# Walking the moving weights of a matmul from the last column to the first in a 256-token decoder trunk

## The chip, the cores and the metric

The kernel runs on one core of one Trainium2 chip. The metric is the device time of one execution in microseconds (us); the median of three runs stands for a kernel. Where single instructions are looked at, times are in nanoseconds (ns). Engines are named as the profile names them: PE is TensorE (matrix multiply), PEld is its weight load, DVE is VectorE, ACT is ScalarE, SP is SyncE, whose queue issues most of the transfers.

## The reference

A decoder trunk of two layers on 256 tokens of width 2048, all in float32. Layer 0 mixes tokens by trailing-window pooling, layer 1 by causal attention over the tokens (with 256 tokens there is one block, so it is plain causal attention). Both have a second branch, a 4-head attention into 256 memory tokens.

```python
for i in range(DEPTH):                                   # 2 layers
    if i == N_A_LAYERS:                                  # before layer 1
        k_blocks, v_blocks, k_mean = moba_shared_kv(h, w_kv_shared)
    u = h @ w_in[i]
    branch_in, gate_b, mem_q, gate_m = jnp.split(u, split_at, axis=-1)
    if i < N_A_LAYERS:
        branch = multiscale_pool(branch_in, pool_w[i], pool_scale[i])
    else:
        branch = moba_attention(branch_in, k_blocks, v_blocks, k_mean)
    mem_o = memory_attention(mem_q, mem, w_mem_kv[i])
    mixed = jnp.concatenate([branch * silu(gate_b), mem_o * silu(gate_m)], axis=-1)
    y = mixed @ w_out[i]
    h = layer_norm(DEEPNORM_ALPHA * h + y, ln_g[i], ln_b[i])
```

## The kernel before

Every float32 factor is split into a high part in the matmul's reduced float32 type and a rest (`split`, lines 70 to 73: ACT writes the high part, DVE the rest). A product is then three matmuls: high by high, high by rest, rest by high. All of them go through the helper `mm` (line 67), so all stand under L68 in the profile and are told apart by their tiles. In a matmul on PE one operand is loaded into the array first (stationary, 128 columns, an LDWEIGHTS of its own on PEld that runs while the matmul before it runs), the other is streamed through it column by column (moving, up to 512 columns), and as many columns of output go to a bank of PSUM.

The weights come from memory in blocks of 128 x 1024 (512 KB), the `items`. `run` (line 131) walks the list of items: it loads an item four ahead, splits it three ahead, and calls its `consume`, which records the matmuls. The order in which the items stand is written out by hand; PE gets one item's matmuls after the other.

There are two kinds of projection:

- `proj_t` (line 168): the weights are stationary (128 columns of `wh` or `wl`), the activations `xT` or `memT` move. Each pair is a matmul of 512 columns (high and rest of the activations side by side) and one of 256. Keys, queries, gates and pool inputs are made this way: 2688 matmuls, `acc<-xm,wh` and `acc<-xm,wl` in the profile.
- `proj_n` (line 194): 128 columns of the activations are stationary, the weights move, 512 columns at a time. Each item gives 12 matmuls (two halves of the tokens, two blocks of the inner dimension, three products). Memory values (`mem_v`), the values of layer 1 (`w_sv`) and the output projections (`w_out`) are made this way.

The last 512 columns of the last output projection are kept in SBUF and multiplied at the end by `last` (line 732), in one pass of 512 columns for the first half of the tokens, and in two of 256 for the second.

Where the operands lie: `xT` and `memT` are parts of one tile `xm`, both shifted by `SHIFT` = 40 columns (160 bytes) against its start. The weights' tiles `wh`, `wl`, the mixed activations `zT`, and the kept columns `kept` (also in `xm`, but from its start) are not shifted. `w_sv` is split into the place of `memT` (`in_mem`, line 651), and so is shifted like `xT`.

By stage, the matmuls with moving weights are:

- `mem_v`, both layers: 192 of 512 columns, stationary `memT` (shifted), moving `wh`, `wl` (not shifted); tiles `xm` with `wh` or `wl`, into `pt`, `o` and `acc`.
- `w_sv`: 288 of 512 columns, stationary `xT` and moving values both in `xm`, both shifted; `acc<-xm`.
- `w_out` of layer 0 (384) and of layer 1 (288), 512 columns, stationary `zT`, moving `wh`, `wl`, neither shifted; `acc<-wh,zT` and `acc<-wl,zT`.
- `last`: 48 of 512 columns and 96 of 256, stationary `zT`, moving `kept`, neither shifted; `acc<-xm,zT`.

Of the kernel before, what the change touches and what calls it, by code (L numbers as in the profile page):

```python
# [20 lines left out]
KT = D // P  # L21
# [25 lines left out]
def trunk(ctx: ExitStack, tc: tile.TileContext, a: dict, out: bass.AP):  # L47
# [11 lines left out]
    kept = [xm[:, i * KX:(i + 1) * KX].rearrange("p (k n) -> p k n", k=KT) for i in range(2)]  # L59
# [7 lines left out]
    def mm(o, l, r, start, stop):  # L67
        nc.tensor.matmul(o, l, r, start=start, stop=stop)  # L68
# [17 lines left out]
    def item(src, cols, consume=None, dst=None):  # L86
        items.append(dict(src=src, cols=cols, consume=consume, dst=dst, cuts=(0, cols)))
# [106 lines left out]
    def proj_n(sta, wblk, done, korder=range(8), banks=("acc", "acc"), place=None):  # L194

        acc = []
        korder = list(korder)

        def consume(j, kb):
            def go(wh, wl):  # L200
                if j == 0:
                    acc.extend(ps.tile([P, 512], F32, name=b, bufs=4 if b == "acc" else 1) for b in banks)
                h = wh.rearrange("p (k n) -> p k n", n=512)
                l = wl.rearrange("p (k n) -> p k n", n=512)
                for t in range(2):
                    for kk in range(2):
                        k = 2 * kb + kk
                        xh = sta[:, k, t * P:(t + 1) * P]
                        xl = sta[:, k, T + t * P:T + (t + 1) * P]
                        first, last = j == 0 and kk == 0, j == 7 and kk == 1  # L210
                        mm(acc[t], xh, h[:, kk], first, False)
                        mm(acc[t], xh, l[:, kk], False, False)
                        mm(acc[t], xl, h[:, kk], False, last)
                    if j == 7:
                        done(t, acc[t])
            return go
        for j, kb in enumerate(korder):
            item(wblk[kb], BLK, consume(j, kb), dst=place and ("keep", *place(j)))
# [34 lines left out]
    def heads_tile(name):  # L253
        return sb.tile([P, 4, 2 * T], F32R, name=name)
# [202 lines left out]
    def fresh(key, make):  # L457

        tiles = []

        def g():
            if not tiles:
                tiles.append(make())
                st[key] = tiles[0]
            return tiles[0]
        return g
# [189 lines left out]
    for grp in range(3):  # L656
        k = fresh("k", lambda: heads_tile("kk"))
# [74 lines left out]
    def last(t, c0, c1):  # L732
        o = ps.tile([P, 512], F32, name="acc", bufs=4)[:, :c1 - c0]
        for k in range(KT):
            zh = zT[:, k, t * P:(t + 1) * P]
            zl = zT[:, k, T + t * P:T + (t + 1) * P]
            mm(o, zh, kept[0][:, k, c0:c1], k == 0, False)
            mm(o, zh, kept[1][:, k, c0:c1], False, False)
            mm(o, zl, kept[0][:, k, c0:c1], False, k == KT - 1)
        return o  # L740

    def add(t, c0, c1, o):
# [21 lines left out]
    def store(t, c0, c1):  # L764
        nc.sync.dma_start(out[t * P:(t + 1) * P, c0:c1], res[:, t, c0:c1])

    o = last(0, 0, 512)
    nc.vector.bn_aggr(m0, stats[:, 1, :3].rearrange("p a b -> p (a b)"))
    for n in (1, 2):
        times_g(n)  # L770
    add(0, 0, 512, o)
    norm_stats(0, 4)
    o = last(1, 0, 256)
    finish(0, 0, 1)
    add(1, 0, 256, o)
    finish(0, 2, 3)
    o = last(1, 256, 512)
# [85 lines left out]
```

## Time and profile before

| | us |
|---|---|
| three runs | 822.35, 823.62, 823.64 |
| median | 823.62 |
| profiled execution | 823.66 |
| its span, first to last instruction | 821.9 |
| PE busy | 812.0 |
| PEld busy | 702.3 |
| DVE busy | 558.5 |
| ACT busy | 396.0 |

A row of the chain of waits has start, duration, engine, tile, line and a count of instructions merged into it. A row of a timeline has start, duration, engine, line, operation, output and inputs, shape and count. The length of one matmul in a row (389 ns for 512 columns) is from its start to the end of its modelled drain; matmuls overlap, so the time that one takes of PE is the distance from one start to the next, called pitch here. It is had from a merged row by dividing its length by its count. A row by windows has for each stretch its length, then for each engine the busy time with the number of instructions that touch it, then the granted TensorE clock (1.00 is full speed), the DMA share and the rate in GB/s.

### The profile page before, as it was taken

To read this page: it belongs to the slowest core of one execution; us is meant where nothing else is said; L and a number is where in the kernel's file an instruction comes from. 1 tells how busy PE (TensorE), PEld (TensorE's weight loads), DVE (VectorE), ACT (ScalarE), POOL (GpSimd) and SP (SyncE) were. 2 spreads that over 40 slices of the span, in tenths; PEclk is the share of its full clock that TensorE was granted. 3 is DMA by queue.
4 is the path that set the end of the run, shared out by engine and by line. 5 is a ranking of instruction groups with operands and counts; after the bars stand their busy time and mean duration, and the time that the engine had idled before them with its cause. 6 is when DMAs were issued, how large, how long until landed. Compare 5 with 4: busy or idle time off the path is not lost.

```text
span 821.9 us, 11533 instructions
## 1 busy us (share of the span) xinstructions
PE 812.0 (99%) x4444; PEld 702.3 (85%) x4444; DVE 558.5 (68%) x794; ACT 396.0 (48%) x578; POOL 0.2 (0%) x4
## 2 busy tenths in 40 slices
PE   9999999999999999999999999999999999999996
PEld 6888898898888888888898888888888888888885
DVE  5686668657957555697667667566765667658746
ACT  6564545545545434445465445454554445545520
POOL 0000000000000000000000000000000000000000
PEclk9999999999999999999999999999999999999998
DMA  8866555557558666676654554656555555637842
GB/s 324 302 232 205 168 165 180 180 163 227 180 176 292 207 201 192 199 237 197 201 157 152 189 170 157 206 158 198 179 166 168 182 188 167 209 127 232 278 130 103
DMA packets 47164, 159.15 MB, mean 194 GB/s; under 512 B 5375, under 2 KB 7167, under 8 KB 46847
## 3 DMA queue, kind: packets, MB, share of 16 engines
q1 hardware_dynamic: 45792, 155.21, 58.0%
q10 hardware_dynamic: 1316, 3.19, 1.0%
q8 instruction: 35, 0.57, 0.3%
q14 instruction: 21, 0.17, 0.1%
HBM read 156.28 MB, written 2.10 MB: 193 GB/s over the span
## 4 chain that ended last, share of the span: by engine, by line
PE 98%; DVE 1%; DMA 0%; ACT 0%; issue 0%; DVEq 0%; SPq 0%
PE acc L68 89%; PE o L68 4%; PE s L68 2%; PE pt L68 2%; PE pt L363 0%; DMA raw<-in_w_mk 0%; PE pt L313 0%; DVE res L806 0%; PE pt L638 0%; PE o L638 0%; DVE res L787 0%; DVE stats L745 0%; DVE res L744 0%; ACT wh L72 0%; DVEq L859 0%
## 5 line engine op out<-in xcount | busy, mean ns | idle before, releaser
L68 PE MATMUL acc<-xm,wh 128*128 128x512 f32 x1344 | 468.7, 395 | 0.5 <-ACT wh L72 0.5
L73 DVE TENSOR_TENSOR wl<-raw,wh 128x1024 fp32r<-128x1024 f32 (+2 forms) x250 | 295.0, 1186 | 150.0 <-ACT wh L72 149.1
L68 PE MATMUL acc<-xm,wl 128*128 128x256 f32 x1344 | 363.3, 280 | 0.0
L72 ACT ACTIVATE wh<-raw 128x1024 fp32r<-128x1024 f32 (+2 forms) x250 | 255.3, 1028 | 187.3 <-PE acc L68 133.3
L68 PEld LDWEIGHTS acc<-xm,wh 128*128 128x128 f32 x1344 | 248.3, 189 | 49.8 <-ACT wh L72 1.5
L68 PEld LDWEIGHTS acc<-xm,wl 128*128 128x128 f32 x1344 | 253.6, 189 | 7.4 <-DVE wl L73 0.4
L68 PE MATMUL acc<-wh,zT 128*128 128x512 f32 x448 | 140.0, 390 | 0.0
L68 PEld LDWEIGHTS acc<-wh,zT 128*128 128x128 f32 x448 | 84.1, 188 | 17.3
L68 PE MATMUL acc<-wl,zT 128*128 128x512 f32 x224 | 87.2, 389 | 0.0
L68 PE MATMUL acc<-xm 128*128 128x512 f32 x288 | 65.8, 389 | 0.0
L68 PEld LDWEIGHTS acc<-xm 128*128 128x128 f32 x288 | 54.1, 188 | 11.2
L73 DVE TENSOR_TENSOR xm<-raw,xm 128x1024 fp32r<-128x1024 f32 (+2 forms) x41 | 47.7, 1171 | 20.6 <-ACT xm L72 20.4
L221 ACT ACTIVATE fold<-acc 128x256 f32<-128x256 f32 x72 | 27.7, 385 | 62.3 <-PE acc L68 61.1
L72 ACT ACTIVATE xm<-raw 128x1024 fp32r<-128x1024 f32 (+2 forms) x41 | 41.3, 1014 | 19.6 <-PE acc L68 9.8
L68 PEld LDWEIGHTS acc<-wl,zT 128*128 128x128 f32 x224 | 42.1, 188 | 8.5
L222 DVE TENSOR_TENSOR fold<-acc,fold 128x256 f32<-128x256 f32 x72 | 29.4, 418 | 5.4 <-ACT fold L221 5.4
L72 ACT ACTIVATE zT<-zf 128x256 fp32r<-128x256 f32 x32 | 12.9, 414 | 39.6 <-DVE zf L283 35.3
L68 PE MATMUL acc<-xm,zT 128*128 128x256 f32 (+1 forms) x144 | 22.6, 318 | 0.0
L68 PEld LDWEIGHTS acc<-xm,zT 128*128 128x128 f32 x144 | 20.7, 190 | 1.9
L68 PE MATMUL acc<-wh,xm 128*128 128x512 f32 x64 | 21.6, 403 | 0.0
L72 ACT ACTIVATE ph<-pt 128x384 fp32r<-128x384 f32 (+1 forms) x20 | 10.7, 535 | 22.2 <-PE pt L363 13.5
L73 DVE TENSOR_TENSOR zT<-zf,zT 128x256 fp32r<-128x256 f32 x32 | 12.8, 422 | 9.7 <-ACT zT L72 9.7
(124 smaller groups left out, 503.6 us busy)
## 6 DMA issues: line engine op xcount, KB each, us to landing
raw<-in_w_in SPq DMA_DIRECT2D x128, 512.0 KB, 3.5
raw<-in_w_out SPq DMA_DIRECT2D x64, 512.0 KB, 4.3
raw<-in_w_sk SPq DMA_DIRECT2D x24, 512.0 KB, 4.5
raw<-in_w_sv SPq DMA_DIRECT2D x24, 512.0 KB, 3.3
raw<-in_w_mv SPq DMA_DIRECT2D x14, 512.0 KB, 5.6
raw<-in_w_mk SPq DMA_DIRECT2D x12, 512.0 KB, 3.3
raw<-in_xT SPq DMA_DIRECT2D x4, 512.0 KB, 4.8
res<-in_x ACTq DMA_DIRECT2D x2, 1024.0 KB, 5.4
```

The lines of the kernel that those rows point to most:

```text
L68: nc.tensor.matmul(o, l, r, start=start, stop=stop)
L72: nc.scalar.activation(hi, src, AF.Copy)
L73: nc.vector.tensor_sub(lo, src, f(hi))
L221: nc.scalar.activation(dst, acc[:, T:], AF.Copy)
L222: nc.vector.tensor_add(dst, acc[:, :T], dst)
```

## The change

In `proj_n` and in `last` the moving operand and the output are given with their columns in reverse: the matmul reads the weights from the last column to the first and writes its output from the last column to the first. Each output column is still the product of the same weight column, and lands at the same address. The stationary operand, the count and the order of the instructions, their waits, and `proj_t` are as before; on every engine the same instructions stand in the same order.

```diff
@@ proj_n, consume
-                        mm(acc[t], xh, h[:, kk], first, False)
-                        mm(acc[t], xh, l[:, kk], False, False)
-                        mm(acc[t], xl, h[:, kk], False, last)
+                        o = acc[t][:, ::-1]
+                        mm(o, xh, h[:, kk, ::-1], first, False)
+                        mm(o, xh, l[:, kk, ::-1], False, False)
+                        mm(o, xl, h[:, kk, ::-1], False, last)
@@ last
-            mm(o, zh, kept[0][:, k, c0:c1], k == 0, False)
-            mm(o, zh, kept[1][:, k, c0:c1], False, False)
-            mm(o, zl, kept[0][:, k, c0:c1], False, k == KT - 1)
+            h, l = (w[:, k, c0:c1][:, ::-1] for w in kept)
+            mm(o[:, ::-1], zh, h, k == 0, False)
+            mm(o[:, ::-1], zh, l, False, False)
+            mm(o[:, ::-1], zl, h, False, k == KT - 1)
```

## Rows read from the trace of the kernel before

**Rows 1.** The page: busy time and share of the span, and the chain by engine.

```profile
PE 812.0 (99%) x4444; PEld 702.3 (85%) x4444; DVE 558.5 (68%) x794; ACT 396.0 (48%) x578; POOL 0.2 (0%) x4
...
PE 98%; DVE 1%; DMA 0%; ACT 0%; issue 0%; DVEq 0%; SPq 0%
```

**Rows 2.** Who waited for whom, PE: waited for, us in total, times, longest.

```profile
PE pt L794 <- DVE cc L791: 2.8, 1, 2.8
PE pt L68 <- DVE zT L126: 1.2, 1, 1.2
PE acc L68 <- ACT wh L72: 0.5, 1, 0.5
PE acc L68 <- ACT cct L796: 0.4, 1, 0.4
```

**Rows 3.** Chain of waits in order of time: output projection of layer 1 and last columns.

```profile
735.09 76.88 PE acc L68 x384
```

**Rows 4.** Busy time by windows, PE alone, inside the 256-column matmuls of `last`.

```profile
802.00:811.00 9.00, 9.00 (x77) 1.00 0.25 93
```

**Rows 5.** Chain of waits: values of layer 1, behind two pieces of `proj_t`.

```profile
505.40 27.35 PE acc L68 x128
...
600.77 27.35 PE acc L68 x128
```

**Rows 6.** Chain of waits: `mem_v` of layer 1, two items and one.

```profile
364.72 5.60 PE acc L68 x24
...
370.76 2.80 PE acc L68 x12
```

**Rows 7.** Chain of waits: `proj_t`, one item and four.

```profile
498.12 2.78 PE acc L68 x16
...
677.40 11.12 PE acc L68 x64
```

**Rows 8.** Timeline of PE, first matmuls of `proj_t` and where their pace changes.

```profile
6.16 0.63 PE L68 MATMUL acc<-xm,wh 128*128 128x512 f32 x1
6.58 0.41 PE L68 MATMUL acc<-xm,wl 128*128 128x256 f32 x1
6.80 0.63 PE L68 MATMUL acc<-xm,wh 128*128 128x512 f32 x1
...
8.72 0.63 PE L68 MATMUL acc<-xm,wh 128*128 128x512 f32 x1
...
10.25 0.28 PE L68 MATMUL acc<-xm,wl 128*128 128x256 f32 x1
10.37 0.39 PE L68 MATMUL acc<-xm,wh 128*128 128x512 f32 x1
```

**Rows 9.** Groups of matmuls with moving weights, shapes apart: busy us, mean ns.

```profile
L68 PE MATMUL acc<-wh,zT 128*128 128x512 f32 x448 | 140.0, 390 | 0.0
L68 PE MATMUL acc<-wl,zT 128*128 128x512 f32 x224 | 87.2, 389 | 0.0
L68 PE MATMUL acc<-xm 128*128 128x512 f32 x288 | 65.8, 389 | 0.0
...
L68 PE MATMUL acc<-xm,zT 128*128 128x256 f32 x96 | 11.7, 283 | 0.0
...
L68 PE MATMUL acc<-xm,zT 128*128 128x512 f32 x48 | 11.0, 389 | 0.0
```

**Rows 10.** Busy time by windows, all engines (PE, PEld, DVE, ACT, POOL): output projection of layer 1.

```profile
735.00:800.00 65.00, 65.00 (x288) 53.83 (x288) 45.28 (x54) 30.30 (x32) 0.00 (x0) 1.00 0.63 210
```

**Rows 11.** Who waited longest between 735 and 800 us.

```profile
ACT wh L72 <- DMA raw<-in_w_out: 12.8, 12, 2.9
```

**Rows 12.** Busy time by windows, PE alone: the highest transfer rate of those read.

```profile
10.00:12.00 2.00, 2.00 (x13) 1.00 1.00 405
```

**Rows 13.** Chain of waits from the last matmul of `last` to the last instruction.

```profile
811.99 0.43 DVE res L744
...
817.94 0.39 DVE res L806
```

## The prediction

> **What bounds the kernel now.** I read the page first: PE is busy for 812.0 us of a span of 821.9, and the chain that ended last is 98% PE [rows 1]. Then the waits: PE waits four times in the whole span, 4.9 us in sum, at its very start and in the tail [rows 2]. So nothing feeds PE too slowly; the time is the sum of the pitches of 4444 matmuls, plus the tail behind the last of them, some 10 us with little PE work in it [rows 13]. The profiled execution took 823.66 us, 1.8 more than its span and 0.04 more than the median of the runs, so a saving in the span is one in the median.
>
> The question is then what sets a pitch. Full speed is 2.4 GHz, a column in 0.417 ns: 512 columns are 213.3 ns and 256 are 106.7. What the rows give:
>
> - 256 columns in the last columns: 77 matmuls touch a stretch of 9.00 us, and each lasts 283 ns, so the pitch is (9.00 + 0.283) / 77 = 120.6 ns; I use 120 [rows 4, 9]. That is 13.3 over the columns.
> - 512 columns in the output projection and the last columns: the row of 384 matmuls holds 288 of 512 columns and these 96; (76.88 - 96 x 0.120) / 288 = 226.9 ns, 13.6 over the columns [rows 3].
> - Values: the row of 128 holds 32 of `proj_t` at 2.78 us for 16, and 96 of the values: (27.35 - 5.56) / 96 = 227.0 ns, 13.7 over [rows 5, 7]. The three groups of heads repeat it.
> - `mem_v`: 5.60 / 24 = 2.80 / 12 = 233.3 ns, 20.0 over [rows 6].
> - `proj_t`, which is not changed: 11.12 / 32 pairs = 347.5 ns for 768 columns (320 ns), 13.75 over for each matmul [rows 7].
>
> So each matmul costs some 13.5 ns more than its columns, and 20 in the one stage where stationary and moving operand are shifted against each other by 160 bytes the unfavourable way. The next view says what kind of cost it is. In the first 10 us the same pairs of `proj_t` run at the lower level: from 6.16 to 8.72 us four pairs start 0.64 us apart, and 768 columns at 1.2 GHz are exactly 640 ns [rows 8]. (The granted clock of those windows reads 1.00, so I go by the pace here.) The excess is then zero. From 10.25 us on it is there. A fixed price for each matmul would show at both levels. What is different at the higher level is that the moving columns are read twice as fast, while the weight load of the next matmul reads SBUF beside them (PEld 53.83 of 65.00 us in the output projection [rows 10]). Together with the 20 against 13.6 ns, which differ by nothing but where the operands lie, I read the excess as two reads in each other's way, a cost that depends on how the two walks meet.
>
> **What the change does, part by part.** No instruction is added, removed or moved, no wait and no transfer changes, and the consumers find the same columns at the same addresses. DVE and ACT have 45.28 and 30.30 us of work in the 65 us of the output projection [rows 10], so they don't become late. The transfers have the thinnest cover: ACT waits there 12.8 us in all for blocks of `w_out`, which PE doesn't feel [rows 11, 2]. A pitch shorter by 3% wants 216 GB/s in place of 210; 405 were moved in another stretch [rows 10, 12]. I cost that at nothing. If the cover were gone, PE would stand still for part of what it gained there, and the waits of PE would say so.
>
> What changes is the pitch of 1200 matmuls of 512 columns (448 + 224 + 288 + 48 in [rows 9], and 192 in `mem_v`) and of 96 of 256. Their whole excess is 1008 x 13.6 + 96 x 13.3 + 192 x 20.0 = 13.7 + 1.3 + 3.8 = 18.8 us. No row shows a reversed walk, so its cost has to be bounded from both sides:
>
> - Best: the two reads no longer meet, as at the lower level, where the excess is zero [rows 8]. Then 18.8 us go: 823.66 - 18.8 = 804.9.
> - Worst of the same kind: every reversed matmul pays what `mem_v` pays now, 6.4 ns more [rows 6]: 1104 x 6.4 = 7.1 us, 830.7.
> - Value taken: the one measured size of an effect of how the walks lie is that 6.4 ns (20.0 - 13.6). I take it as a gain on each of the 1296: 8.3 us, so 815.4. It is nearer the middle of the bounds than either end.
>
> Why a gain and not a loss: in all geometries that are not shifted the unfavourable way the excess is the same 13.3 to 13.75, whichever tile, shape and stage [rows 3, 4, 5, 7]. A pattern of meetings that no address changes much is what two walks give that cross each other all the way, whatever their offset. If the weight load goes through its 128 columns from the last to the first, which no row shows, the moving walk crosses it now and runs along with it after the change. Of two walks in one direction, one of them twice as fast, fewer lines coincide. That is an argument, not a row, and so the chances stay wide.
>
> [...] The rows show a full-rate matmul with a weight load beside it at 226.9 ns, and the excess gone when the columns come at half the rate [rows 3, 8]. [...]
>
> **The rivals.**
>
> 1. No change. The excess is a price of full speed that has nothing to do with addresses, and only `mem_v` comes down from 20.0 to 13.6, or not even that: 0 to 192 x 6.4 = 1.2 us, 822.4 to 823.7. For it: 13.5 ns in five geometries [rows 3 to 5, 7]. Against it: zero at the lower level, and 20.0 in `mem_v` [rows 6, 8]. A program that still walked forwards would end here too.
> 2. Slower by meetings. Place: the same 1104 matmuls of output projections, values and last columns, which now lie well. Reversed, the moving walk starts from the other end of its 512 columns, and the two reads meet as in `mem_v`: 6.4 ns each, 830.7. It decides from the point where the reversed pitch passes the 227 ns of now: each ns more over the 1296 is 1.3 us. For it: `mem_v` shows that a worse meeting exists [rows 6]. Against it: it would have to hit aligned and shifted stages alike.
> 3. Half rate. Reading or writing backwards breaks the pairing of neighbouring columns, and a column takes two ticks: as at the lower level [rows 8], 1200 x 213.3 + 96 x 106.7 ns = 266 us more, 1090. No row has an output or a moving operand that isn't walked forwards, so only its size speaks against it. [...]
>
> **How the numbers follow.** About 0.2%, 1.65 us, is what a measurement of this kernel can tell from no change. Chances: faster by fewer meetings (forecast) 0.45; no change 0.30; slower by meetings 0.19; half rate 0.06. The predicted time is that of the likeliest, 815.4. That case by itself reaches from 804.9 to 822. The range is 808 to 831: it takes in no change and the slower case at its full price of 830.7. Left out are half rate (0.06), a slower case beyond `mem_v`'s price (some 0.05) and the best end below 808 (some 0.05). Faster 0.45, within 0.2% 0.30, slower 0.25.
>
> **What would show it.** In the profile after, the row of 384 matmuls from `w_out` to the last columns (76.88 us now) should be about 74.4; the 96 matmuls of the values 21.2 in place of 21.8; an item of `mem_v` 2.72 in place of 2.80; and a pair of `proj_t` still 347.5 ns, which is the check that nothing else moved. A row of 76.9 and 2.80 says no change; 2.72 with 76.9 says that only the shifted stage gained. Rows of 79.3 and more say rival 2; rows of 140 and more say rival 3. PE should go on waiting only where it waits now; a new wait for `wh` in the output projection of layer 1 would mean that the transfers' cover is gone. The prediction is wrong in its reading, whatever its number, if the pitch of the 256-column matmuls doesn't move with that of the 512-column ones, since the weight load lies beside both in the same way.

## The result and the profile after

The change made the kernel slower: 828.57 us in the median of four runs (828.27 to 828.84) against 822.99 of the kernel before (821.96 to 823.64, four runs with the three shown ahead), a ratio of 1.0072 with a 95% interval of 1.006 to 1.0085. The profiled execution took 828.78 us with a span of 827.0.

The chain of waits in order of time of the kernel after (start, duration, what, count), the rows that answer to [rows 3, 5, 6, 7]:

```profile
365.95 5.60 PE acc L68 x24
...
487.96 11.12 PE acc L68 x64
...
506.69 27.97 PE acc L68 x128
...
738.44 78.63 PE acc L68 x384
```

The memory values (5.60 for 24) and `proj_t` (11.12 for 64) are as they were. The row with the 96 matmuls of the values grew from 27.35 to 27.97, so their pitch went from 227.0 to (27.97 - 5.56) / 96 = 233.4 ns. The row of the output projection and the last columns grew from 76.88 to 78.63. Shapes apart, in groups of the same profile (busy us, mean ns of one):

```profile
L68 PE MATMUL acc<-wh,zT 128*128 128x512 f32 x448 | 143.2, 398 | 0.0
L68 PE MATMUL acc<-wl,zT 128*128 128x512 f32 x224 | 89.0, 398 | 0.0
L68 PE MATMUL acc<-xm 128*128 128x512 f32 x288 | 67.7, 397 | 0.0
...
L68 PE MATMUL acc<-xm,zT 128*128 128x256 f32 x96 | 11.5, 282 | 0.0
...
L68 PE MATMUL acc<-xm,zT 128*128 128x512 f32 x48 | 11.4, 397 | 0.0
```

All groups of 512 columns grew against [rows 9]; the one of 256 columns shrank, from 11.7 to 11.5. The last record of such a row lasts 0.28 us, 0.16 more than its pitch of 0.12; without these 0.16 us, the 96 pitches are (11.7 - 0.16) / 96 = 120 ns before and (11.5 - 0.16) / 96 = 118 after. The 288 matmuls of 512 columns in the last row of the chain then have (78.63 - 96 x 0.118) / 288 = 233.7 ns.

The sum by stages: 1008 matmuls x 6.4 ns = 6.5 us more, 96 x 1.7 ns = 0.2 us less, 6.3 in all. The two profiled spans are 5.1 apart. The rest is in the first 12 us, before any changed matmul: in the profiled execution of before PE runs at the lower pace until 10 us [rows 8], in that of after a pair of `proj_t` takes 0.35 us already at 6 us:

```profile
5.95 0.40 PE L68 MATMUL acc<-xm,wh 128*128 128x512 f32 x1
...
6.30 0.40 PE L68 MATMUL acc<-xm,wh 128*128 128x512 f32 x1
```

That gave this execution some 1.3 us which lie ahead of the first changed matmul: in the chain the first memory values start at 13.31 us before and at 11.99 after, and from there to the last matmul of `last` it is 798.7 us before and 805.1 after, 6.4 more. The medians are 5.6 apart; the four runs of before lie at 821.96 and 822.35 and at 823.62 and 823.64, so that a difference of medians is uncertain by about 1 us, and in what follows small differences are read from rows.

PE waits no longer than before in the output projection, and for no transfer there; its only new wait is one of 0.2 us for `wl` at the start.

### The profile page after: what moved, and what is told of

It reads as the page before. It is cut to its first block, busy times and chain, and to the rows that moved or that the text cites. A ratio compares the mean times of both kernels' runs of the same rounds, so it can differ in the third digit from the quotient of the medians.

```text
span 827.0 us, 11532 instructions
## 1 busy us (share of the span) xinstructions
PE 817.1 (99%) x4444; PEld 701.0 (85%) x4444; DVE 558.5 (68%) x794; ACT 395.6 (48%) x578; POOL 0.2 (0%) x4
## 4 chain that ended last, share of the span: by engine, by line
PE 98%; DVE 1%; DMA 1%; SPq 0%; ACT 0%; issue 0%; DVEq 0%
PE acc L68 89%; PE o L68 4%; PE s L68 2%; PE pt L68 2%; DMA raw<-in_w_mk 1%; PE pt L364 0%; PE pt L314 0%; SPq L99 0%; DVE res L808 0%; PE pt L639 0%; PE o L639 0%; DVE res L789 0%; DVE wl L73 0%; ACT wh L72 0%; DVE stats L747 0%
## 5 line engine op out<-in xcount | busy, mean ns | idle before, releaser
L68 PE MATMUL acc<-wh,zT 128*128 128x512 f32 x448 | 143.2, 398 | 0.0
L68 PE MATMUL acc<-wl,zT 128*128 128x512 f32 x224 | 89.0, 398 | 0.0
L68 PE MATMUL acc<-xm 128*128 128x512 f32 x288 | 67.7, 397 | 0.0
L72 ACT ACTIVATE ph<-pt 128x384 fp32r<-128x384 f32 (+1 forms) x20 | 10.7, 535 | 22.3 <-PE pt L364 13.5
```

What stands on the lines that cost most here:

```text
L72: nc.scalar.activation(hi, src, AF.Copy)
```

## The experiments

After the result, three theories stood. A: the read of the moving operand meets the read of the next weights, and a backwards walk meets it worse. B: writing PSUM backwards is dearer. C: a reversed walk has a fixed price at its start.

### Which of the two operands: `e1_move_only` and `e2_out_only`

The changed kernel with one of the two reversals taken back.

```diff
@@ e1_move_only (in proj_n; the same in last)
-                        o = acc[t][:, ::-1]
+                        o = acc[t]
@@ e2_out_only (in proj_n; the same in last)
-                        mm(o, xh, h[:, kk, ::-1], first, False)
+                        mm(o, xh, h[:, kk], first, False)
```

> The changed kernel with the moving operand reversed and the output walked forwards, so the columns of these products come out mirrored; the work is the same. Theory A (reads meet): all of the loss is here, 828.6 us, 512-column pitch 233.3. Theory B (writing PSUM backwards): 823, pitch 227.

> The changed kernel with the output reversed and the moving operand walked forwards, mirrored products again, same work. Theory A (reads meet): 823, pitch 227 with 233.3 left in the memory values as before. Theory B (writing PSUM backwards): 828.6, pitch 233.3.

Measured: with the moving operand alone reversed 828.87 us, ratio to the kernel before 1.0067 (1.005 to 1.0084); with the output alone reversed 822.41, ratio 0.9996 (0.9987 to 1.0005). The row of 384 matmuls in the chain, first of the one and then of the other:

```profile
738.40 78.63 PE acc L68 x384
```

```profile
734.92 76.87 PE acc L68 x384
```

The whole loss is in the read of the moving operand (78.63 against 76.88); theory B falls. A backwards walk over adjoining columns of PSUM cost nothing here (76.87 against 76.88).

### The pitch by form: `m1_dirs`

The kernel before with 24 blocks of 20 extra matmuls behind the last one, each block on a line of its own; the form of a line (this is the one with both reversed):

```diff
+    for i in range(20): nc.tensor.matmul(bo[:128, :512][:, ::-1], zf[:, 512 * (i % 15) + 0:512 * (i % 15) + 128], xm[:, 512 * (i % 15) + 0:512 * (i % 15) + 512][:, ::-1], start=i == 0, stop=i == 19)
```

> The kernel before, with 24 blocks of 20 extra matmuls each behind the last matmul of the last columns, operands from SBUF as they lie there (stationary from the mixed activations, moving from the kept columns, no relative shift), output to a PSUM bank that nobody reads. Each block has one form: 512, 448, 384, 320, 256, 128 columns, walked forwards or backwards, the moving operand and the output also reversed one at a time, and the stationary operand cut to 64, 32 and 8 columns. The time of the whole is not compared; the pitch of each block is read. Theory A (the read of the moving operand meets the read of the next weights): forwards 512 columns 227 ns, both reversed 233.3; moving operand alone reversed 233.3; output alone reversed 227. With fewer stationary columns the excess over the columns falls with their number, at 64 to about half (220 and 223), at 8 to nearly nothing (214 to 216), and forwards and backwards become equal. Theory B (the write to PSUM backwards is dearer): output alone reversed 233.3, moving alone 227, and the 6.4 ns stay with 8 stationary columns. Theory C (a fixed price of starting a reversed walk): the difference between backwards and forwards is the same 6.4 ns at 512, 384 and 256 columns; by what the changed kernel's last columns show (118.3 against 120) it should already be minus 1.7 at 256.

The chain of waits of this kernel; a twentieth of a row's duration is a pitch. L781 to L784 have 512 columns: forwards, moving reversed, output reversed, both. L785 to L788 are the same four with 256 columns, L789 and L790 have 384 forwards and both reversed. L793 and L794 have 64 stationary columns, forwards and both reversed, L797 and L798 have 8. L803 and L804 are the forms of L781 and L784 again, with every matmul a sum of its own.

```profile
810.98 4.56 PE s L781 x20
815.54 4.67 PE s L782 x20
820.21 4.55 PE s L783 x20
824.76 4.67 PE s L784 x20
829.43 2.39 PE s L785 x20
831.83 2.37 PE s L786 x20
834.20 2.39 PE s L787 x20
836.59 2.37 PE s L788 x20
838.96 3.47 PE s L789 x20
842.42 3.56 PE s L790 x20
...
850.39 4.60 PE s L793 x20
854.99 4.67 PE s L794 x20
...
868.95 4.62 PE s L797 x20
873.58 4.67 PE s L798 x20
...
892.29 4.53 PE s L803 x20
896.83 4.67 PE s L804 x20
```

Three readings. First, 228 and 233.5 ns, about as in the kernel, and 226.5 and 233.5 in L803 and L804. A difference of that size stands without transfers too: in `m3_more` a backwards walk costs 5 ns more (L811 and L812 below) where the DMA share is 0.00 (925 to 935 us). Second, backwards costs 5.5 ns more at 512 columns, 4.5 at 384 (178.0 against 173.5), and 1 ns less at 256 (118.5 against 119.5): not a fixed price, theory C falls. The columns themselves are counted at 0.417 ns here, as in the prediction. No view names that figure; it is an estimate, half of the lower pace's 640 / 768 = 0.833 ns [rows 8]. The steps from 256 to 512 columns forwards give 0.415 ns a column in the kernel before (226.9 - 120.6 = 106.3 ns) and 0.424 in these blocks (228 - 119.5 = 108.5 ns). And at the end of the kernel before, where the granted clock reads 0.50 (815.6 to 817 us), two matmuls of 512 columns start 0.42 us apart (815.91 and 816.33). Over the columns, so counted, backwards is 11.8 ns at 256, 18.0 at 384, 20.2 at 512: it grows with the columns. Forwards it is 12.8, 13.5 and 14.7. The blocks of 320 and 448 columns, not shown, fit in: 13.7 and 19.8 backwards, 13.2 and 16.3 forwards. So backwards it grows by some 8 ns from 256 to 512 columns, forwards by 2 to 4. Third, theory A falls in the form that I gave it. With 8 stationary columns the weight load shrinks to a record of 88 ns in place of 188:

```profile
L797 PEld LDWEIGHTS s<-xm,zT x20: 87/88/93, 868.6 to 873.0; 128*8 128x8 f32 x20
```

By theory A both directions should have come to 214 to 216. Backwards stayed at 233.5, and forwards *rose* from 228 to 231. So the price is not simply the weight load in the way of the moving operand. In these blocks a matmul of 512 columns costs 231 to 233.5 ns in all forms but the forwards walk beside the load of 64 or 128 columns, which costs 226.5 to 230.

### Where the operands lie: `m2_offs`

The same kind of blocks, with the stationary operand 0 to 112 columns off the moving operand's alignment.

> The kernel before, with 34 blocks of 20 extra matmuls in the same place; the stationary operand starts 0 to 112 columns (0 to 448 bytes) off the moving operand's alignment, forwards and backwards, at 512 columns and for some offsets at 256. Theory A (two reads meet): forwards the pitch depends on the offset, between 227 (at 0) and 233 or more (at 40, as the memory values had it), with at least one offset at each; backwards it depends on the offset too, and some offset brings it to 227 or below. Theory C or B (a price of the reversed walk itself, of its start or its write): backwards 233.3 at every offset. The changed kernel's memory values, 233.3 with an offset of 40 as the others have at 0, speak for a backwards walk that doesn't depend on the offset.

Chain of waits; each odd line is forwards, the even line behind it the same backwards. Offsets in columns: L781 0, L785 8, L795 40, L799 64, L801 96.

```profile
810.44 4.56 PE s L781 x20
815.00 4.67 PE s L782 x20
...
829.01 4.66 PE s L785 x20
833.67 4.67 PE s L786 x20
...
875.75 4.67 PE s L795 x20
880.42 4.68 PE s L796 x20
...
894.36 4.57 PE s L799 x20
898.94 4.67 PE s L800 x20
...
903.61 4.65 PE s L801 x20
908.26 4.79 PE s L802 x20
```

Forwards, 0 columns give 228.0 by this row, 64 give 228.5 and 8, 40 and 96 give 232.5 to 233.5; of the offsets not shown 48 and 112 lie at 229.5, and 4, 12, 16, 24 and 32 at 233 to 234.5. Backwards it is 233.5 to 234 at ten of twelve offsets, 236.5 at 32 and 239.5 at 96; none is favourable. The weight load's own record doesn't tell the offsets apart: in the kernel before it is 188 ns in the output projections, in line, and 188 to 189 in the memory values, 40 off. At 256 columns the directions differ by 2 ns at most, at five offsets. So the statement became: **512 columns of float32 cost about 233 ns in either direction; forwards, with the stationary operand in line or at one of a few other offsets (48, 64 and 112 columns here), they cost 227 to 230.**

### In the kernel: `e3_zT_shifted`, `e5_zT_alone`, `e6_both`

If that is right, forwards walks must become as slow as the change when the mixed activations `zT` are moved out of line.

```diff
@@ e3_zT_shifted
-    zT = sb.tile([P, KT, 2 * T], F32R, name="zT")
+    zT = sb.tile([P, KT * 2 * T + SHIFT], F32R, name="zT")[:, SHIFT:].rearrange("p (k t) -> p k t", k=KT)
@@ e5_zT_alone (e6_both: the same in the changed kernel)
-    zT = sb.tile([P, KT, 2 * T], F32R, name="zT")
+    zT = sb.tile([P, KT * 2 * T + 128], F32R, name="zT")[:, SHIFT:SHIFT + KT * 2 * T].rearrange("p (k t) -> p k t", k=KT)
```

> The kernel before, every walk forwards, but the mixed activations, stationary in the output projections and last columns, start 40 columns later in their tile, as the memory activations do. Nothing else is changed. If 227 is a favourable case that needs the stationary operand in line with the moving one, and 233.3 the ordinary price in either direction, the 672 matmuls of the output projections and the 48 of 512 columns in the last columns go to 233.3: 720 x 6.5 ns = 4.7 us more, 828.1, without any reversed walk; the values (288) stay at 227. If the direction itself is what costs, nothing changes: 823.4.

`e3_zT_shifted` came out at 828.33 us, as expected and for the wrong reason. The tile grew by 160 bytes, and every tile behind it, the weights among them, moved along, so the output projection stayed in line while `proj_t` and the memory values changed their offset. Its chain of waits:

```profile
77.52 11.31 PE acc L68 x64
...
366.01 5.47 PE acc L68 x24
...
738.61 77.21 PE acc L68 x384
```

`proj_t` went from 347.5 to 11.31 / 32 = 353.4 ns for a pair, the memory values came down from 233.3 to 227.9, and the row of 384 only grew by the 48 wide matmuls of the last columns, which did go out of line. The same rule, at other places than meant, though not evenly: three pieces of 64 matmuls of `proj_t` in layer 1 only went from 11.12 to 11.16 us, and why they lost less stays open. The next two runs move `zT` alone.

> The kernel before, all walks forwards, with the mixed activations 40 columns later in their tile and the tile 512 bytes longer, so that all tiles behind it keep their place modulo 512 bytes (in the run with a shifted zT they moved by 160 bytes along with it, so output projections stayed in line and the stages with stationary weights went out of line instead). If forwards is cheap only in line: 672 + 48 matmuls go from 226.9 to 233.3, 4.6 to 4.7 us more, 827.9, values and pairs of proj_t unchanged. If the direction alone is what costs: 823.2.

> The changed kernel with the same shift of the mixed activations. If a backwards walk pays its 233.3 at this offset as at offset 0, the two don't add: 828.6, as the changed kernel. If backwards walk and shift are two prices: 833.

`e5_zT_alone`, all walks forwards: 827.93 us, ratio 1.0053 (1.0038 to 1.0068). `e6_both`, shifted and backwards: 828.02, ratio 1.0065 (1.0048 to 1.0082). Rows of the chain of the first, then of the second:

```profile
77.39 11.12 PE acc L68 x64
...
506.08 27.35 PE acc L68 x128
...
735.97 78.78 PE acc L68 x384
```

```profile
506.36 27.97 PE acc L68 x128
...
738.12 78.58 PE acc L68 x384
```

Without one reversed walk the output projection costs 78.78 us, as much as the change made it (78.63), while values and `proj_t`, which the shift doesn't touch, keep 27.35 and 11.12. And with both, the two prices don't add: 78.58. So the loss of the change is the loss of the favourable case.

### The change in part: `e4_part`

```diff
+                        w = -1 if sta is memT else 1
+                        o = acc[t][:, ::w]
+                        mm(o, xh, h[:, kk, ::w], first, False)
@@ last
+            s = -1 if c1 - c0 < 512 else 1
```

The edit, shortened; `s` is used in `last` as `w` is here.

> The change in part: only the memory values (stationary operand shifted by 40 columns already) and the 256-column passes of the last columns walk backwards; values and output projections forwards. If the loss lies only where the stationary operand is in line with the moving one and 512 columns move: 192 x 0 and 96 x -1.6 ns = 0.2 us less, no change that can be measured, 823.2. If every reversed matmul of 512 columns pays 4 to 6 ns: 0.8 to 1.2 us more.

Measured 822.28, ratio 0.9999 (0.9989 to 1.0008). Its memory values and its row of 384:

```profile
365.14 5.60 PE acc L68 x24
...
735.57 76.83 PE acc L68 x384
```

Reversal costs nothing in the memory values, whose operands are out of line already (5.60 as before), nor where only 256 columns move (76.83 against 76.88).

### What the 20 ns belong to: `m3_more` and `m4_low`

> The kernel before, with more blocks of extra matmuls behind the last columns, output again to a bank that nobody reads. (a) Both operands shifted by 8 columns, and the moving operand alone by 40, forwards and backwards. (b) Matmuls on bfloat16 copies: 512 columns side by side (2 bytes a column), and 512 columns with every second one taken (4 bytes a column, as float32 has), forwards and backwards. (c) Pairs of 512 and 256 columns as the stages with stationary weights have them, at 16 offsets. (d) Four backwards and four forwards in the tail, where the clock is granted at 0.50. Theory A' (a backwards walk of 512 float32 columns pays 20 ns at full speed because of how fast lines of SBUF are wanted, and forwards in line with the weight load is the one favourable case): (a) both shifted alike 227 forwards, 233 backwards; (b) side by side 216 to 219 forwards and backwards alike, every second column 227 to 233 as float32; (d) 427 forwards and backwards, the price is zero. Theory C' (a price of a backwards walk as such): (b) 6 ns between backwards and forwards in bfloat16 too; (d) 6 ns there too, 433. (c) is a search: 347.5 ns is what the kernel has at 40 columns, 344 is the sum of the best seen of either length.

> The kernel before with the eight warm-up matmuls at its start made float32 of 512 columns (on zeros, output not read): four backwards, then four forwards. PE runs there at 427 ns for 512 columns. If the price of a backwards walk belongs to the full pace of the columns, both read 427 ns. If it is a price of the backwards walk in time, the first four read 433 or more.

In part (a) of `m3_more` L783 and L784 have both operands shifted by 8 columns, forwards and backwards:

```profile
810.28 4.54 PE s L783 x20
814.82 4.67 PE s L784 x20
```

That is 227 and 233.5 ns, as without a shift; what counts is where one operand lies against the other. Of the rows not shown, with the moving operand alone shifted by 40 it is 234.5 and 233.5; with 384 columns and the stationary operand 40 off it is 176.5 in both directions.

L809 to L812 are bfloat16 matmuls of 512 columns: columns side by side forwards and backwards, then every second column forwards and backwards. In its chain of waits:

```profile
920.17 4.26 PE s L809 x19
924.43 4.32 PE s L810 x20
928.75 2.25 PE s L811 x10
...
931.06 2.19 PE s L811 x9
933.25 4.60 PE s L812 x20
```

One record is missing in L809 and one in L811. Side by side, 2 bytes a column, it is 216 ns in both directions (4.32 / 20 backwards; forwards the 4.26 us hold 19 records of 0.379 us each, (4.26 - 0.379) / 18). With every second column taken, 4 bytes a column as in float32, it is 225 forwards (from 928.75 to 933.25 us, 4.50 / 20) and 230 backwards. In these blocks a backwards walk is free where columns are 2 bytes apart and costs 5 ns where they are 4 bytes apart; in the second pair the moving operand's start alternates by 64 columns, so the offset was not held. The kernel's float32 form stood at 226.9 before the change. What in the reading of SBUF makes the second pair dearer, 225 against 216 ns, no run here shows.

Part (d) of `m3_more` missed: PE was at the full pace there, its matmuls some 0.23 us apart. `m4_low` did it at the start. L129 are the backwards ones (the last two of four), L130 the forwards ones, in timelines of PE from 2.7 to 3.2 us and from 0 to 7 us:

```profile
2.46 1.05 PE L129 MATMUL pt<-zT 128*128 128x512 f32 x2
...
3.31 1.91 PE L130 MATMUL pt<-zT 128*128 128x512 f32 x4
```

One record lasts 0.63 us at that pace [rows 8], so the pitch is 1.05 - 0.63 = 0.42 and (1.91 - 0.63) / 3 = 0.43 us. The two backwards pitches from 2.46 to 3.31 us make 0.85, where 433 ns each would make 0.87. So it is 427 ns, 512 columns at the 0.833 ns of [rows 8], in either direction (the granted clock reads 1.00 in this stretch too, so the level is taken from the pace). With the operands in line, the price of the walk shows only at the full pace of the columns.

Part (c) of `m3_more` has pairs of 512 and 256 columns, the moving operand shifted by 0 to 120 columns in steps of 8. At 0, 8, 40, 72 and 104 columns a pair takes 346.7 to 347.5 ns, at the eleven other offsets 350.8 to 353.3; with both walks reversed it takes 350.8 to 353.3 at all four offsets tried. The kernel's `proj_t`, 347.5 with a shift of 40, stands at a favourable offset for such pairs, though rows of 512 columns alone are not favourable there: nothing to gain.

### A version made from this: `b1_memT`

The memory activations moved by 88 columns, in line with the weights where they are stationary, and the 256-column passes backwards.

```diff
+    place_v, memT = memT, xm[:, 128 + KX:128 + 2 * KX].rearrange("p (k t) -> p k t", k=KT)
-        return [memT[:, 4 * (j % 4) + ...
+        return [place_v[:, 4 * (j % 4) + ...
```

The reversal in `last`, as in `e4_part`, is left out here.

> A version made by what the runs before showed. All 512-column walks forwards; the memory activations moved by 88 columns, so that they are in line with the weights when they are stationary; the 256-column passes of the last columns backwards. Theory (in line is cheap, out of line 233): memory values from 233.3 to 227 to 228, 192 x 5.5 to 6.3 = 1.1 to 1.2 us less, the 256-column passes 0.16 us less. The memory keys, 128 pairs in which the memory activations move, go from 40 columns off to in line, which cost proj_t 353 in place of 347.5 ns when the weights moved: 0.7 us more. Sum 0.4 to 0.7 us less, 823.0 against 823.5, at or under what can be measured. If alignment is not what it is: no change at all in the memory values.

Measured 822.82 against 822.49 (medians), ratio 0.9994 (0.9985 to 1.0003): no difference that can be told. Its memory values did come down:

```profile
364.88 5.50 PE acc L69 x24
```

229.2 in place of 233.3 ns, 0.8 us over 192 matmuls, and short of the 227 to 228 expected. The memory keys gave most of it back: a row of 32 in the chain went from 5.55 to 5.64 us, 5.6 ns for a pair, some 0.7 us over 128 pairs. From the first memory values to the last matmul the chain has 798.2 us in place of 798.7. No version was found that is measurably faster than the kernel before.

## Why the prediction was wrong

It forecast 815.4 us, faster; the kernel became slower, 828.57, inside the range of 808 to 831. The case that came was rival 2, with a chance of 0.19: the reversed stages pay what the memory values paid already.

- *PE bounds the kernel, and only the pitches of moving weights change.* Right. `proj_t` kept 11.12, PE's waits stayed, the cover of the transfers held.
- *The size, 6.4 ns a matmul, from 20.0 against 13.6.* Right to some tenths: 233.4 in the values and 233.7 in the last row after, against 227.0 and 226.9. Rival 2 at 830.7 was too dear by the 256-column passes, which gained 1.7 ns each where it let them lose, and by the start of the profiled execution, 1.3 us shorter ahead of every changed instruction.
- *The sign.* Wrong, and this is the step that failed: "I take it as a gain on each of the 1296". It stood on the sentence that the excess is "the same 13.3 to 13.75, whichever tile, shape and stage", in five geometries. They were not five. Values have both operands shifted by 40 columns, output projections have neither, and the last columns, wide and narrow, are in line too: one relative offset, zero, seen four times. The fifth, `proj_t`, has its moving operand shifted by 40, which part (c) of `m3_more` shows to be one of the five favourable of sixteen offsets; and its 13.75 is half a pair's excess, not the excess of a matmul. The only other offset of a 512-column walk in the same kind of stage, the memory values, stood at 233.3. `m2_offs` shows that of twelve offsets eight cost 232.5 or more forwards. What I took for the ordinary price, with the memory values as the bad exception, was the favourable case, and the memory values were ordinary. From a favourable case a blind change of the walk leads more likely to the ordinary one.
- *Two reads in each other's way.* Wrong as told. That the excess vanishes at the lower pace was a right reading of [rows 8], and `m4_low` repeats it backwards. But a longer weight load was not what made it dear: with 8 of its 128 columns left (`m1_dirs`, a record of 88 in place of 188 ns) the pitch rose to 231. The place of the stationary operand does act on the pitch, as `m2_offs` and `e5_zT_alone` show; whether that is a help at some offsets or a hindrance at the others the runs don't tell. Backwards the price was there at every offset tried. The place of the stationary operand alone moves the pitch by some 6 ns: by (78.78 - 76.88) / 288 = 6.6 in the last row of `e5_zT_alone`, from 228 to 233.5 at 40 columns in `m2_offs`.
- *The 256-column test.* The prediction said that its reading is wrong if the pitch at 256 columns doesn't go with that at 512. It went the other way (118 from 120), and the reading was wrong.
- *No change and half rate.* Neither came. Writing PSUM backwards has no price (76.87 against 76.88 us), and reading SBUF backwards one of 3% (233.4 and 233.7 against 227.0 and 226.9 ns at 512 columns). A pairing of neighbouring columns, on which half rate stood, was the author's assumption; no run shows one.

What stays open: why a forwards walk with the stationary operand in line escapes the cost that grows with the columns, what sets the favourable offsets, and what makes every second bfloat16 column dearer than columns side by side (225 against 216 ns forwards). The stationary operand's own walk was not varied.

## What to carry to other kernels

Before a price is called ordinary, count the different conditions in which it was seen: four stages with the same relative alignment are one observation. Where a pitch depends on where operands lie, a change of walk or place should be measured against several offsets in a row of short blocks, which one run can hold, before it goes into the kernel; and a tile that grows moves all tiles behind it, so the offset that changes may be another than the one meant.

## What the runs showed of the hardware

- A matmul of 512 float32 columns with 128 stationary ones, at full pace: 233.5 to 234 ns backwards at ten of twelve offsets (236.5 and 239.5 at the two others), 226.5 to 234.5 forwards, depending on the offset (`m1_dirs`, `m2_offs`). In bfloat16 with columns side by side 216 in both directions (`m3_more`). At the lower pace, in line, 427 in both directions (`m4_low`).
- Reversing the output in PSUM is free (76.87 against 76.88 us for the row of 384 matmuls; ratio of the times 0.9996; `e2_out_only`).
- Backwards at 256 columns is not dearer by more than 0.5 ns, mostly 1 to 2 cheaper (118.5 against 119.5 in line by rows of blocks); in line it is 4.5 dearer at 384 columns, and 5.5 to 7 at 512 (`m1_dirs`, `m2_offs`).
- A shorter weight load made the forwards matmul of 512 columns slower, not faster: 230 ns with 64 stationary columns, 231 with 8, 228 with 128, in line (`m1_dirs`).
